# Decoder block on one core: small pads that shift where tiles start within a partition of the on-chip memory

## Chip, cores and metric

The kernel runs on one core of one Trainium2 chip. The time is device microseconds of that core, the median of several executions. The profile is one profiled execution of the same program; its span goes from the first to the last instruction.

## What is computed

A decoder block in float32 over 256 tokens of width 2048: a gated feed-forward layer of width 5632, a token-mixing part (differential attention beside a gated linear recurrence, merged by gates), a second feed-forward layer, and a gated per-layer embedding. Cut to the products that matter for the time:

```python
x = x + 0.5 * swiglu(rmsnorm(x, ffn1_norm), w_gate1, w_up1, w_down1)
h = rmsnorm(x, mix_norm)
dq, dk, dv, hq, hf, hi, hg, gate_a, gate_b = split(h @ w_in)
y_a = diff_attention(dq, dk, dv, ...)
y_b = hgrn2(hq, hf, hi, hg, ...)
merged = sigmoid(gate_a) * (y_a @ w_branch_a) + sigmoid(gate_b) * (y_b @ w_branch_b)
x = x + merged @ w_out
x = x + 0.5 * swiglu(rmsnorm(x, ffn2_norm), w_gate2, w_up2, w_down2)
x = x + sigmoid(rmsnorm(x, ple_gate_norm) @ w_ple_gate) * rmsnorm(p @ w_ple_proj, ple_post_norm)
```

## The kernel before

All weights come once from the main memory, in one stream of 805 groups of two k-tiles (a tile of 128 rows by 512 columns each), in the order of use. `prep` (L101) loads a group into `raw` by a DMA from SP's queue (L112), rounds it on ScalarE into `wh` (L114) and puts the rest, `raw - wh`, into `wl` on VectorE (L115). It runs three groups ahead of the matmuls.

The activations lie transposed, features on partitions, and are split into a rounded and a rest part in the same way: `AH, AL` (16 k-tiles of 256 tokens) after each norm, `hH, hL` for the hidden layer, `yaH, yaL` and `ybH, ybL` for the two branches, `mH, mL` for the merged branch, `pH, pL` for the embedding. `group` (L141) multiplies a group: for each of its two k-tiles and each half of the tokens three matmuls of 128x128 by 128x512. The activation is the **stationary** operand, which a weight load brings into the array, and the weight tile is the **moving** one:

```python
hi, lo = AH[:, kt, tcol(tt)], AL[:, kt, tcol(tt)]
nc.tensor.matmul(dst, hi, wh[:, k2, cols], start=(kt == 0), stop=False)    # L148
nc.tensor.matmul(dst, hi, wl[:, k2, cols], start=False, stop=False)        # L149
nc.tensor.matmul(dst, lo, wh[:, k2, cols], start=False, stop=(kt == last)) # L150
```

So a group is 12 matmuls. In the profile a matmul is listed as out<-moving,stationary: `acc<-wh,AH` is L148 with `AH` stationary. Between two groups of the stream `advance` (L129) issues one piece of every side task: transposes and splits of the hidden layer (L259 to L269), the residual and its transposes (L228), the attention heads, the recurrence (whose small float32 matmuls stand at L589, L616, L629 and L638 to L641).

The order on every engine is that in which the code is written. Tiles are taken from pools; where a tile lies is fixed by the sizes of the tiles allocated before it, each rounded up to 32 bytes, so that the sizes of small tiles decide at what byte the large ones begin. Of the tiles that the three matmuls read, these are the addresses (bytes within a partition, as the built program has them) and what they leave when divided by 128:

| tile | role | address before | mod 128 |
|---|---|---|---|
| `wh` (4 buffers, 4096 bytes apart) | moving | 93248 | 64 |
| `wl` (4 buffers, 4096 bytes apart) | moving | 109632 | 64 |
| `AH`, `AL` | stationary | 34816, 51200 | 0, 0 |
| `hH`, `hL` | stationary | 126016, 171072 | 64, 64 |
| `yaH`, `yaL` | stationary | 150592, 158784 | 64, 64 |
| `ybH`, `ybL` | stationary | 175200, 183392 | 96, 96 |
| `mH`, `mL` | stationary | 191584, 207968 | 96, 96 |
| `pH`, `pL` | stationary | 136256, 138304 | 64, 64 |

The 128 columns of one stationary operand are 512 bytes, and consecutive ones lie 512 bytes apart; a moving operand is 2048 bytes. So each operand has the remainder of its tile.

Of the kernel before, what the change touches and what calls it, by code (L numbers as in the profile page):

```python
# [20 lines left out]
P = 128  # L21
# [27 lines left out]
def block_kernel(ctx: ExitStack, tc: tile.TileContext, a: dict, out: bass.AP):  # L49
# [3 lines left out]
    base = ctx.enter_context(tc.tile_pool(name="base", bufs=1))  # L53
# [8 lines left out]
    def T(pool, shape, tag, dt=F32, **kw):  # L62
        uid[0] += 1
        return pool.tile(shape, dt, tag=tag, name=f"{tag}_{uid[0]}", **kw)
# [4 lines left out]
    def ccol(c):  # L69
        return slice(c * NB, (c + 1) * NB)  # L70

# [1 line left out]
    plan = []  # L73

    def add(w, chunks, groups):
# [39 lines left out]
            nc.vector.tensor_tensor(wl[:, ks, :], raw[:, ks, :], wh[:, ks, :].bitcast(F32), op=ALU.subtract)  # L115
        ready[n] = (wh, wl)

# [1 line left out]
    tasks = []  # L119
    owed = [False]  # L120

# [55 lines left out]
                group(at[0] + i, act, 2 * groups - 1, [d])  # L177
            yield d

# [1 line left out]
    def split(H, L, src, gain=None):  # L181
        if gain is None:
            nc.scalar.copy(H, src)  # L183
            nc.vector.tensor_tensor(L, src, H.bitcast(F32), op=ALU.subtract)  # L184
        else:
            nc.scalar.activation(H, src, AF.Copy, scale=gain)  # L186
            nc.vector.scalar_tensor_tensor(L, src, gain, H.bitcast(F32), op0=ALU.mult, op1=ALU.subtract)
# [34 lines left out]
    def new_act():  # L222
        return T(base, [P, KD, SEQ], "AH", F32R), T(base, [P, KD, SEQ], "AL", F32R)

    def new_ss4():
        return T(base, [P, NT, 4], "ss4", bufs=2)
# [20 lines left out]
    def ffn(gu, down, act, gain_next):  # L247
        with tc.tile_pool(name=gu, bufs=1) as fp:
            hH = T(fp, [P, DFF // P, SEQ], "hH", F32R)
            hL = T(fp, [P, DFF // P, SEQ], "hL", F32R)  # L250

            def hidden(acc, c):
                if c == 0 and rs[0] is None:
                    early = T(fp, [P, NT, NB], "early")
                    for tt in range(NT):
                        nc.scalar.copy(early[:, tt, :], acc[tt])
                    acc = [early[:, tt, :] for tt in range(NT)]
                while rs[0] is None:
                    yield  # L259
                h = []  # L260
                for tt in range(NT):
                    s = T(fp, [P, HALF], "s", bufs=2)
                    nc.scalar.activation(s, acc[tt][:, :HALF], AF.Silu, scale=rs[0][:, tt : tt + 1])  # L263
                    h.append(T(fp, [P, HALF], "h", bufs=4))
                    nc.vector.scalar_tensor_tensor(  # L265
                        h[tt], acc[tt][:, HALF:], rs[0][:, tt : tt + 1], s, op0=ALU.mult, op1=ALU.mult
                    )
                yield
                two_k_tiles(lambda tt, kt: h[tt][:, (kt - 2 * c) * P : (kt - 2 * c + 1) * P], hH, hL, 2 * c)  # L269

            for c in range(DFF // HALF):
                acc = product(gu, c, KG, act)
                spawn(hidden(acc, c))
            nact = new_act()
            ss4 = new_ss4()
            for c in range(D // NB):
                acc = product(down, c, FG, (hH, hL))
                spawn(residual(acc, c, 0.5, ss4, nact, gain_next, set_rs if c == 3 else None))
        return nact

    # ------------------------------------------------------------------ first FFN
    gains = T(base, [P, 4, KD], "gains")
    nc.sync.dma_start(gains, a["gains"])
    neghalf = T(base, [P, 16], "neghalf")
# [7 lines left out]
    small = T(base, [P, 4], "small")  # L292
    ident = T(base, [P, P], "ident")
    x = T(base, [P, NT, D], "x")
    act = new_act()
    ss4 = new_ss4()

    def load_xT(g):
# [26 lines left out]
    spawn(first_sums())  # L325
    act = ffn("gu1", "down1", act, gains[:, G_MIX])

    # ------------------------------------------------------------------ token mixing
    mid = ctx.enter_context(ExitStack())
    mp = mid.enter_context(tc.tile_pool(name="mid", bufs=1))  # L330
    GA = T(mp, [P, NT, D], "GA")
    V = T(mp, [P, NT, NH * VD], "V")
    yaH = T(mp, [P, NH, SEQ], "yaH", F32R)
    yaL = T(mp, [P, NH, SEQ], "yaL", F32R)
    gsub = T(mp, [P, 1], "gsub")
    nc.vector.tensor_scalar(gsub, small[:, S_SUB : S_SUB + 1], 1.0 - LAMBDA_INIT, None, op0=ALU.mult)

    def mix(m):
# [27 lines left out]
    with tc.tile_pool(name="att", bufs=1) as ap:  # L366
        qT = T(ap, [P, NH, SEQ], "qT")
        kT = T(ap, [P, NH, SEQ], "kT")
        dv = T(ap, [P, NT, NH * VD], "dv")
        bias = T(ap, [P, NH, SEQ], "bias")  # L370
# [55 lines left out]
                yield  # L426
            have.add(key)

        # the queries of a tile stand in reversed order from qT to aT, as the rows of the bias do
        PARTS = ((0, slice(0, SEQ), slice(0, SEQ)), (1, slice(SEQ, 3 * P), slice(P, SEQ)))  # L430

        def head(h, ya):
# [304 lines left out]
            spawn(residual(acc, c, 1.0, ss4, act, gains[:, G_FFN2], set_rs if c == 3 else None))  # L737
    mid.close()

    # ------------------------------------------------------------------ second FFN  # L740
    act = ffn("gu2", "down2", act, gains[:, G_PLE])

    # ------------------------------------------------------------------ per-layer embedding
    with tc.tile_pool(name="ple", bufs=1) as pp:
        pT = T(pp, [P, 2, SEQ], "pT")
        nc.gpsimd.dma_start(pT, a["pT"])
# [49 lines left out]
        drain()  # L796


# [1 line left out]
def _blocks(w):  # L800
    k, n = w.shape
    return np.ascontiguousarray(w.reshape(k // (2 * P), 2, P, n // NB, NB).transpose(3, 0, 2, 1, 4))


def _gate_up(gate, up):
    k, n = gate.shape
    both = np.stack([gate.reshape(k, n // HALF, HALF), up.reshape(k, n // HALF, HALF)], axis=2)
    return _blocks(both.reshape(k, 2 * n))


def _feature_major(w):
    n, m = w.shape
    return np.ascontiguousarray(w.reshape(n // P, P, m).transpose(1, 0, 2))
# [12 lines left out]
def _constants():  # L826
    j = np.arange(TOEP)
    dist = SEQ - 1 - j
    hot = np.zeros((BUCKETS + 1, TOEP), np.float32)
    ok = dist >= 0  # L830
    hot[_buckets(dist)[ok], j[ok]] = 1.0
    hot[BUCKETS, ~ok] = NEG
    s = np.arange(P)[:, None]
    t = np.arange(64)[None, :]
    masks = np.stack([(s // (2 * m) == t // m) & (s % (2 * m) < m) for m in LEVELS], axis=1).astype(np.int32)
    return hot, masks


def _layout(v):
    v = {k: np.asarray(w) for k, w in v.items()}  # L840
    hot, masks = _constants()
    f = lambda w: np.ascontiguousarray(w)  # noqa: E731
    x = v["x"][0]
    gains = np.stack([v[n][0].reshape(KD, P).T for n in ("ffn1_norm", "mix_norm", "ffn2_norm", "ple_gate_norm")], axis=1)
    small = np.stack(
        [np.tile(v["q_norm"][0], 2), np.tile(v["k_norm"][0], 2), v["diff_subln"][0], v["hgrn_norm"][0]], axis=1
    )
    return {
        "xT": _feature_major(f(x.T)),
        "x": f(x),  # L850
        "pT": _feature_major(f(v["p"][0, 0].T)),
        "gains": f(gains),
        "small": f(small),
        "ident": np.eye(P, dtype=np.float32),
        "flip": f(np.eye(P, dtype=np.float32)[::-1]),
        "rel_bias": f(v["rel_bias"]),
        "onehot": hot,
        "masks": masks,
        "lambdas": f(np.stack([v[n][0] for n in ("lambda_q1", "lambda_q2", "lambda_k1", "lambda_k2")])),
        "lb": f(v["hgrn_lb_logits"].reshape(2, NH, P).transpose(2, 0, 1)),  # L860
        "ple_post": f(v["ple_post_norm"][0]),
        "gu1": _gate_up(v["ffn1_w_gate"][0], v["ffn1_w_up"][0]),
        "down1": _blocks(v["ffn1_w_down"][0]),
        "w_in": _blocks(v["w_in"][0]),
        "w_a": _blocks(v["w_branch_a"][0]),
        "w_b": _blocks(v["w_branch_b"][0]),
        "w_out": _blocks(v["w_out"][0]),
        "gu2": _gate_up(v["ffn2_w_gate"][0], v["ffn2_w_up"][0]),
        "down2": _blocks(v["ffn2_w_down"][0]),
        "w_pg": _blocks(v["w_ple_gate"][0]),  # L870
        "w_pp": _blocks(v["w_ple_proj"][0]),
    }


def build(arrays):
    import concourse.bacc as bacc

    nc = bacc.Bacc("TRN2", target_bir_lowering=False, num_devices=1)
    aps = {
        n: nc.dram_tensor(f"in_{n}", w.shape, mybir.dt.from_np(w.dtype), kind="ExternalInput").ap()  # L880
        for n, w in arrays.items()
    }
    out = nc.dram_tensor("out_y", (SEQ, D), F32, kind="ExternalOutput").ap()
    with tile.TileContext(nc) as tc:
        block_kernel(tc, aps, out)
    return nc
# [9 lines left out]
```

## Time and profile before

| | before |
|---|---|
| median of 3 executions | 2321.66 us |
| lowest, highest | 2320.70, 2322.68 us |
| profiled execution, first to last instruction | 2320.3 us |
| TensorE (PE) matmul busy | 2312.7 us |
| weight loads (PEld) busy | 1903.2 us |
| VectorE (DVE) busy | 1270.9 us |
| ScalarE (ACT) busy | 1042.7 us |
| GpSimd (POOL) busy | 39.5 us |

For the profiled execution only its span is known; the median of the runs lies 1.4 us above it. The table of stages below comes from the timeline: when the first matmul with each stationary operand of the stream begins.

| first matmul at, us | stationary | product |
|---|---|---|
| 5.51 | AH, AL | first gate and up |
| 502.91 | hH, hL | first down |
| 745.77 | AH, AL | mixing input, with attention and recurrence beside it |
| 1200.30 | yaH, yaL | branch a |
| 1248.84 | AH, AL and ybH, ybL in turn | gate b and branch b, four times |
| 1385.75 | mH, mL | mixing output |
| 1478.82 | AH, AL | second gate and up |
| 1972.69 | hH, hL | second down |
| 2215.52 | AH, AL, twice pH, pL | embedding gate and embedding |

Matmuls are pipelined, and the recorded duration of one runs past the start of the next. The pace is therefore read from the distance between starts, not from the durations.

### The profile page before, as it was taken

The numbers are of one execution on the slowest core, as the hardware profiler recorded it, in microseconds if no ns is written. First come the engines' busy times: TensorE is split into PE (matmuls) and PEld (weight loads), VectorE is DVE, ScalarE is ACT, GpSimd is POOL, SyncE is SP. The second block draws the span as 40 slices with busy tenths as digits, with TensorE's granted clock in tenths as the row PEclk, the third lists the DMA queues.
The fourth block names the chain that finished last, engine by engine and source line by source line (L and its number), as shares of the span: only waits on it lengthen the run. The fifth ranks groups of instructions, "written<-read, shape, count | busy, mean of one in ns | idle before, by whom it ended". The sixth has DMA issues, their size and how long they took to land.

```text
span 2320.3 us, 27206 instructions
## 1 busy us (share of the span) xinstructions
PE 2312.7 (100%) x10564; PEld 1903.2 (82%) x10564; DVE 1270.9 (55%) x1381; ACT 1042.7 (45%) x1270; POOL 39.5 (2%) x38
## 2 busy tenths in 40 slices
PE   9999999999999999999999999999999999999999
PEld 7888888888888888888888888888888888888887
DVE  5554555554444576667765555555555554444456
ACT  6444444444444455543344444544444444444454
POOL 0000000000000100000010000000000000000000
PEclk9999999999999999999999999999999999999999
DMA  8655555566666645554455655565555556666664
GB/s 292 190 182 191 190 188 185 189 189 188 188 188 196 201 161 167 186 173 153 160 156 181 186 186 181 179 193 184 189 190 185 188 188 190 193 188 191 188 213 149
DMA packets 120464, 432.55 MB, mean 186 GB/s; under 512 B 13773, under 2 KB 14181, under 8 KB 120208
## 3 DMA queue, kind: packets, MB, share of 16 engines
q1 hardware_dynamic: 118800, 426.33, 58.3%
q0 software_dynamic: 1248, 4.43, 0.5%
q8 instruction: 82, 1.34, 0.2%
q14 instruction: 46, 0.38, 0.0%
q10 hardware_dynamic: 288, 0.07, 0.0%
HBM read 428.67 MB, written 2.11 MB: 186 GB/s over the span
## 4 chain that ended last, share of the span: by engine, by line
PE 99%; DMA 1%; DVE 0%; ACT 0%; SPq 0%; issue 0%; ACTq 0%; DVEq 0%
PE acc L148 32%; PE acc L150 31%; PE acc L149 31%; PE tp L209 1%; PE ms L616 1%; DMA raw<-in_gu 0%; PE tp L219 0%; PE ms L440 0%; PE ms L150 0%; PE ms L149 0%; PE ms L148 0%; PE ms L589 0%; PE tp L362 0%; DMA junk<-in_xT 0%; PE tp L477 0%; PE ms L641 0%
## 5 line engine op out<-in xcount | busy, mean ns | idle before, releaser
L115 DVE TENSOR_TENSOR wl<-raw,wh 128x1024 fp32r<-128x1024 f32 (+1 forms) x805 | 983.9, 1223 | 888.9 <-ACT wh L114 886.5
L114 ACT CAST wh<-raw 128x1024 fp32r<-128x1024 f32 (+1 forms) x805 | 844.9, 1051 | 941.1 <-PE acc L150 915.6
L148 PE MATMUL acc<-wh,AH 128*128 128x512 f32 x2224 | 885.2, 398 | 0.2 <-ACT wh L114 0.2
L150 PE MATMUL acc<-wh,AL 128*128 128x512 f32 x2224 | 872.3, 392 | 0.0
L149 PE MATMUL acc<-wl,AH 128*128 128x512 f32 x2224 | 866.9, 390 | 1.6 <-DVE wl L115 1.6
L150 PEld LDWEIGHTS acc<-wh,AL 128*128 128x128 f32 x2224 | 417.7, 188 | 95.5
L149 PEld LDWEIGHTS acc<-wl,AH 128*128 128x128 f32 x2224 | 418.1, 188 | 91.5 <-DVE wl L115 3.7
L148 PEld LDWEIGHTS acc<-wh,AH 128*128 128x128 f32 x2224 | 418.4, 188 | 84.7 <-ACT wh L114 1.7
L148 PE MATMUL acc<-wh,hH 128*128 128x512 f32 x704 | 275.3, 391 | 0.0
L150 PE MATMUL acc<-wh,hL 128*128 128x512 f32 x704 | 274.2, 390 | 0.0
L149 PE MATMUL acc<-wl,hH 128*128 128x512 f32 x704 | 273.9, 389 | 0.0
L150 PEld LDWEIGHTS acc<-wh,hL 128*128 128x128 f32 x704 | 132.1, 188 | 27.8
L149 PEld LDWEIGHTS acc<-wl,hH 128*128 128x128 f32 x704 | 132.2, 188 | 27.1
L148 PEld LDWEIGHTS acc<-wh,hH 128*128 128x128 f32 x704 | 132.2, 188 | 27.1
L263 ACT ACTIVATE s<-acc,rowr 128x256 f32<-128x256 f32 x86 | 40.8, 477 | 49.9 <-PE acc L150 49.9
L183 ACT CAST hH<-tp 128x512 fp32r<-128x512 f32 x44 | 25.8, 587 | 74.7 <-PE tp L209 74.7
L184 DVE TENSOR_TENSOR hL<-tp,hH 128x512 fp32r<-128x512 f32 x44 | 30.4, 692 | 46.6 <-ACT hH L183 46.5
L265 DVE SCALAR_TENSOR_TENSOR h<-acc,rowr,s 128x256 f32<-128x256 f32 x86 | 41.4, 483 | 20.6 <-ACT s L263 20.6
L148 PE MATMUL acc<-wh,mH 128*128 128x512 f32 x128 | 51.3, 401 | 0.0
L149 PE MATMUL acc<-wl,mH 128*128 128x512 f32 x128 | 50.6, 395 | 0.0
L150 PE MATMUL acc<-wh,mL 128*128 128x512 f32 x128 | 50.6, 395 | 0.0
L186 ACT ACTIVATE AH<-tp,gains 128x256 fp32r<-128x256 f32 x48 | 22.9, 477 | 31.0 <-PE tp L209 16.9
(191 smaller groups left out, 1019.9 us busy)
## 6 DMA issues: line engine op xcount, KB each, us to landing
raw<-in_gu SPq DMA_DIRECT2D x351, 512.0 KB, 3.5
raw<-in_down SPq DMA_DIRECT2D x176, 512.0 KB, 3.8
raw<-in_w_in SPq DMA_DIRECT2D x176, 512.0 KB, 3.6
raw<-in_w_out SPq DMA_DIRECT2D x32, 512.0 KB, 3.7
raw<-in_w_pg SPq DMA_DIRECT2D x32, 512.0 KB, 4.3
raw<-in_w_a SPq DMA_DIRECT2D x16, 512.0 KB, 3.5
raw<-in_w_b SPq DMA_DIRECT2D x16, 512.0 KB, 3.5
junk<-in_xT SPq DMA_DIRECT2D x8, 256.0 KB, 4.2
```

The lines of the kernel that those rows point to most:

```text
L114: nc.scalar.copy(wh[:, ks, :], raw[:, ks, :])
L115: nc.vector.tensor_tensor(wl[:, ks, :], raw[:, ks, :], wh[:, ks, :].bitcast(F32), op=ALU.subtract)
L148: nc.tensor.matmul(dst, hi, wh[:, k2, cols], start=(kt == 0), stop=False)
L149: nc.tensor.matmul(dst, hi, wl[:, k2, cols], start=False, stop=False)
L150: nc.tensor.matmul(dst, lo, wh[:, k2, cols], start=False, stop=(kt == last))
L183: nc.scalar.copy(H, src)
L184: nc.vector.tensor_tensor(L, src, H.bitcast(F32), op=ALU.subtract)
L186: nc.scalar.activation(H, src, AF.Copy, scale=gain)
L209: nc.tensor.transpose(tp[:, i, tcol(tt)], src_of(tt, kt + i), ident)
L263: nc.scalar.activation(s, acc[tt][:, :HALF], AF.Silu, scale=rs[0][:, tt : tt + 1])
L265: nc.vector.scalar_tensor_tensor(h[tt], acc[tt][:, HALF:], rs[0][:, tt : tt + 1], s, op0=ALU.mult, op1=ALU.mult)
L616: nc.tensor.matmul(lp[:, i, tt, :], km[:, i, tt, :], q4[:, i, tt, :], start=True, stop=True)
```

## The change

A tile of 64 bytes is allocated ahead of `AH, AL` and another one behind them, and nothing reads or writes them. `gsub`, one value per partition, takes a tile of 128 bytes of which one column is used. The other lines of the diff take comments out.

```diff
@@ -292,7 +292,9 @@
     ident = T(base, [P, P], "ident")
     x = T(base, [P, NT, D], "x")
+    T(base, [P, 16], "lead")
     act = new_act()
+    T(base, [P, 16], "trail")
     ss4 = new_ss4()
@@ -325,14 +327,14 @@
     yaL = T(mp, [P, NH, SEQ], "yaL", F32R)
-    gsub = T(mp, [P, 1], "gsub")
+    gsub = T(mp, [P, 32], "gsub")[:, 0:1]
     nc.vector.tensor_scalar(gsub, small[:, S_SUB : S_SUB + 1], 1.0 - LAMBDA_INIT, None, op0=ALU.mult)
```

Names apart, the instructions of every engine and their order stay the same. The addresses become:

| tile | before, mod 128 | after | after, mod 128 | distance to `wh`, mod 512, before | after |
|---|---|---|---|---|---|
| `wh` | 64 | 93376 | 64 | | |
| `wl` | 64 | 109760 | 64 | | |
| `AH`, `AL` | 0 | 34880, 51264 | 64 | 448 | 384 |
| `hH`, `hL` | 64 | 126144, 171200 | 64 | 0 | 0 |
| `yaH`, `yaL` | 64 | 150720, 158912 | 64 | 0 | 0 |
| `ybH`, `ybL` | 96 | 175424, 183616 | 64 | 32 | 128 |
| `mH`, `mL` | 96 | 191808, 208192 | 64 | 32 | 128 |
| `pH`, `pL` | 64 | 136384, 138432 | 64 | 0 | 0 |

The last two columns are the address of the stationary tile less that of `wh`, divided by 512; `wl` lies 16384 bytes behind `wh`, and every step from operand to operand is a multiple of 512, so the remainder is the same for all matmuls of a row.

Of the small float32 matmuls, the recurrence's stationary tiles `k`, `km`, `A` and `off` go from 0 to 96 (and their moving `q`, `qm` from 0 to 96 too, while `V` stays at 64), `qT` and `kT` from 96 to 64, `aT` from 32 to 0 and its moving `dv` from 96 to 64. `x` and `ident`, which the transposes read, stay at 0.

## The prediction

> **What bounds the kernel now.** I read first the page's busy shares, the clock and the chain of work that ended last, to see which engine sets the end.
>
> ```profile
> span 2320.3 us, 27206 instructions
> PE 2312.7 (100%) x10564; PEld 1903.2 (82%) x10564; DVE 1270.9 (55%) x1381; ACT 1042.7 (45%) x1270; POOL 39.5 (2%) x38
> ...
> PEclk9999999999999999999999999999999999999999
> ...
> q1 hardware_dynamic: 118800, 426.33, 58.3%
> ...
> PE 99%; DMA 1%; DVE 0%; ACT 0%; SPq 0%; issue 0%; ACTq 0%; DVEq 0%
> ```
>
> TensorE is busy from end to end at the full granted clock, and 99% of the chain is its own work. VectorE stands at 55%, ScalarE at 45%, the weight queue at 58.3% of the DMA engines. The end moves only if the matmuls follow each other at another pace. Next, the costliest groups, for the kinds of matmul and whether they wait.
>
> ```profile
> L115 DVE TENSOR_TENSOR wl<-raw,wh 128x1024 fp32r<-128x1024 f32 (+1 forms) x805 | 983.9, 1223 | 888.9 <-ACT wh L114 886.5
> L114 ACT CAST wh<-raw 128x1024 fp32r<-128x1024 f32 (+1 forms) x805 | 844.9, 1051 | 941.1 <-PE acc L150 915.6
> L148 PE MATMUL acc<-wh,AH 128*128 128x512 f32 x2224 | 885.2, 398 | 0.2 <-ACT wh L114 0.2
> L150 PE MATMUL acc<-wh,AL 128*128 128x512 f32 x2224 | 872.3, 392 | 0.0
> L149 PE MATMUL acc<-wl,AH 128*128 128x512 f32 x2224 | 866.9, 390 | 1.6 <-DVE wl L115 1.6
> L150 PEld LDWEIGHTS acc<-wh,AL 128*128 128x128 f32 x2224 | 417.7, 188 | 95.5
> ...
> L150 PEld LDWEIGHTS acc<-wh,hL 128*128 128x128 f32 x704 | 132.1, 188 | 27.8
> ...
> L148 PE MATMUL acc<-wh,mH 128*128 128x512 f32 x128 | 51.3, 401 | 0.0
> ```
>
> Three things are to be seen. The matmuls hardly wait for another engine (0.2 and 1.6 us in all). ScalarE's casts wait for TensorE to release `wh` (915.6 us), so the suppliers are ahead. And the recorded 390 to 401 ns of a matmul is no pace, since 6672 of them alone would exceed the span: they overlap. A weight load is recorded with 188 ns whether it reads `AL` (remainder 0) or `hL` (64), so a load's own duration doesn't tell an address apart either.
>
> The pace has to come from starts. The timeline of TensorE gives the starts of single matmuls. I took stretches with nothing but the three lines of the stream, one for each kind of stationary operand, and show the first and last row of each; the remainder of the operand's address is in the tables above.
>
> ```profile
> 259.63 0.40 PE L149 MATMUL acc<-wl,AH 128*128 128x512 f32 x1
> ...
> 281.15 0.39 PE L150 MATMUL acc<-wh,AL 128*128 128x512 f32 x1
> ...
> 509.76 0.39 PE L149 MATMUL acc<-wl,hH 128*128 128x512 f32 x1
> ...
> 547.84 0.39 PE L149 MATMUL acc<-wl,hH 128*128 128x512 f32 x1
> ...
> 1221.48 0.39 PE L149 MATMUL acc<-wl,yaH 128*128 128x512 f32 x1
> ...
> 1248.26 0.39 PE L150 MATMUL acc<-wh,yaL 128*128 128x512 f32 x1
> ...
> 1272.27 0.40 PE L148 MATMUL acc<-wh,ybH 128*128 128x512 f32 x1
> ...
> 1283.24 0.40 PE L150 MATMUL acc<-wh,ybL 128*128 128x512 f32 x1
> ...
> 1415.72 0.40 PE L149 MATMUL acc<-wl,mH 128*128 128x512 f32 x1
> ...
> 1434.86 0.39 PE L150 MATMUL acc<-wh,mL 128*128 128x512 f32 x1
> ...
> 2243.87 0.39 PE L148 MATMUL acc<-wh,AH 128*128 128x512 f32 x1
> ...
> 2265.62 0.39 PE L150 MATMUL acc<-wh,AL 128*128 128x512 f32 x1
> ```
>
> From first to last start, divided by the steps between them:
>
> - `AH` (remainder 0): 95 starts, 21.52 us / 94 = 228.9 ns; in the last stage 96 starts, 21.75 / 95 = 228.9 ns.
> - `hH` (64): 169 starts, 38.08 / 168 = 226.7 ns.
> - `yaH` (64): 119 starts, 26.78 / 118 = 226.9 ns.
> - `ybH` (96): 48 starts, 10.97 / 47 = 233.4 ns.
> - `mH` (96): 83 starts, 19.14 / 82 = 233.4 ns.
>
> ```profile
> 1200.30:1248.80 48.50, 48.50 (x238) 40.86 (x237) 31.07 (x48) 18.93 (x21) 8.21 (x4) 1.00 0.56 173
> 1272.20:1283.40 11.20, 11.20 (x50) 9.02 (x49) 5.12 (x5) 5.06 (x6) 0.00 (x0) 1.00 0.62 185
> ```
>
> These are two windows, of `yaH` and of the first `ybH`: the stretch, its length, the busy time of PE, PEld, DVE, ACT and POOL, the granted clock, the DMA engines' share and GB/s.
>
> So the kernel before already holds an experiment. Shape, types, code lines and moving tiles are the same throughout; the pace falls into three classes, and they go with the remainder: 226.8, 228.95 and 233.4 ns. It isn't the stage: `AH` has one pace beside the hidden layer's work at 260 us and in the quiet stage at 2244 us, while `yaH` and `ybH`, 50 us apart at the same clock, differ by 6.5 ns, and the faster one has the busier neighbour (VectorE 31.07 of 48.5 us against 5.12 of 11.2).
>
> **The change, part by part.** No instruction is added, removed or moved; only starting bytes differ. Each term is a count of matmuls by a difference of pace.
>
> 1. `AH, AL` go from 0 to 64. Three rows of x2224 are 6672 matmuls. If they take the pace of the class at 64, each gains 228.95 − 226.8 = 2.15 ns: **14.3 us**.
>
> ```profile
> L150 PE MATMUL acc<-wh,ybL 128*128 128x512 f32 x64 | 25.3, 396 | 0.0
> ```
>
> 2. `mH, mL` (three lines of x128, 384) and `ybH, ybL` (three of x64, 192) go from 96 to 64: 576 × 6.6 ns = **3.8 us**.
>
> 3. `hH`, `yaH`, `pH` stay at 64, and `wh`, `wl` with them: **nothing**.
>
> 4. The start. In the chain of waits the first groups stand behind their loads:
>
> ```profile
> 5.78 5.35 DMA raw<-in_gu
> ...
> 12.74 5.56 DMA raw<-in_gu
> ```
>
> Up to about 18 us the pace is that of the DMA, and some 60 matmuls gain nothing: 60 × 2.15 ns = **0.1 us** off the sum, 0.2 with the waits just behind.
>
> 5. The small float32 matmuls of recurrence and attention change their remainders, some to 96. The trace of before doesn't show them there.
>
> ```profile
> L616 PE MATMUL ms<-qm,km 128*128 128x64 f32 x192 | 22.7, 271 | 0.0
> ...
> L589 PE MATMUL ms<-q,k 128*128 128x128 f32 x32 | 4.2, 274 | 0.0
> ...
> L477 PE MATMUL tp<-dv,aT 128*128 128x128 f32 x16 | 3.1, 275 | 0.0
> L641 PE MATMUL ms<-V,A 128*128 128x128 f32 x16 | 3.1, 275 | 0.0
> ```
>
> With the other groups of this kind (32 more at L616, 64 at L629 to L641, 16 more with `aT`) they are some 350. If each lost what the worst class of the stream loses against the best, 6.6 ns, that is 2.3 us; if each gained it, −2.3 us. Their recorded durations lie within 271 to 275 ns whether their operands now stand at 0 and 0, at 0 and 64, or at 32 and 96, which is nearest to **no change**: I take 0 and keep both ends.
>
> 6. The 96 narrower matmuls of the last product (L148 to L150 into `ms`, 256 columns) also read `AH, AL`. Bounds are none and the full 2.15 ns, 0.2 us; I take none.
>
> Sum: 14.3 + 3.8 − 0.2 = 17.9 us. The profiled execution would go from 2320.3 to 2302.4 us, and the median, 1.4 us above the span now as then, from 2321.7 to **2303.8 us** (0.8% less).
>
> What is late next? A group takes TensorE 12 × 228.95 = 2.75 us and would take 2.72. The cast takes 1.05 us (L114) and the rest 1.22 (L115) of that, and the queue needs 58.3% of the DMA engines, so the cover stays: nothing that feeds the stream is near its limit. If it were gone, the gain would turn into waits at L148 and L149, which now have 1.8 us.
>
> [...]
>
> **The rivals.**
>
> *The pace follows the distance between stationary and moving operand, with a period longer than 128 bytes* (slower). In the table all operands of the fast class lie at a distance from `wh` that is 0 modulo 512, not only modulo 128. `AH` goes from 448 to 384, `mH` and `ybH` from 32 to 128; none of them reaches 0. With a period of 256 or 512 they may land on a bad distance. The worst pace seen is 233.4 ns; at that, `AH` loses 4.45 ns × 6672 = 29.7 us, and `mH`, `ybH` stay as they are: 2351 us. It is slower as soon as `AH`'s runs lie above 228.95 ns by more than the 0.57 ns that the second term pays for (3.8 us / 6672). For it: the trace has no pair at 128 or 384. Against it: within a class consecutive operands differ by multiples of 512 without a difference in pace, so no longer period than 512 is possible, and the two slow classes differ as much by absolute remainder as by distance; 128 is the shortest period that tells all three apart.
>
> *The same, but neutral for `AH`*: at 384 it keeps 228.95 ns, while `mH` and `ybH` leave the worst place and reach 226.8 to 228.95. The gain is 576 × 4.45 to 6.6 ns = 2.6 to 3.8 us: 2318 to 2319 us, within what can't be told from no change.
>
> *Addresses don't matter; the class is of the product*, by its surrounding work or how its operand was written. Then nothing moves: 2321.7 us. For it: each product has one pace only. Against it: `yaH`, `pH` and `hH` come from three kinds of work and have one pace, `ybH` and `mH` another. [...]
>
> *The second term alone fails, or the first is only halved* (a partial effect at the new distances): 2307 to 2311 us.
>
> **How the numbers follow.** Forecast 0.79, 2303.8 us. Slower by a longer period 0.05; neutral for `AH` 0.08; no effect of addresses 0.04; partial 0.04. Its own bounds: per matmul the classes are known to about 0.1 ns from each side, so the first term is 6672 × 1.95 to 2.25 = 13.0 to 15.0 us and the second 3.7 to 3.9; with the ends of part 5 the gain is 14.2 to 21.4 us. That is 2300.3 to 2307.5 us. To leave out no more than 2 in 10 the range takes the near end of the partial case: 2300 to 2308.5 us. About 0.2% (4.6 us) is what a measurement of this kernel can tell from no change. Faster by more: the forecast and the partial case, 0.83. Within: the neutral case and no effect, 0.12. Slower: 0.05.
>
> **What would show it.** In the changed kernel's timeline, stretches of the stream between two transposes should give 226.6 to 227.0 ns per start for `AH`, `mH` and `ybH` as for `hH`, and `hH` itself should stay. The waits at L148 and L149 should stay near 2 us and the granted clock at full. The slower case shows as `AH` above 229 ns, the neutral one as `AH` at 228.9 with `mH` faster; a pace of 226.8 without a shorter span would mean that the gain turned into a wait. If starts at L589 to L641 stood further apart than before, by 6.6 ns each, part 5 would sit at its upper end.

## Result and profile after

The changed kernel takes 2347.39 us (median of 4 runs, 2345.69 to 2347.81) against 2321.53 us before: a ratio of 1.0108, with a 95% interval of 1.0096 to 1.0120. The forecast was 2303.8 us. It went the other way, and close to the first rival (2351 us). Two of the ten executions of one experiment below, `e4_gsub_only`, took 4715 and 10792 us, its profiled one among them, so that paces aren't read from its trace.

The page of the changed kernel, in the order in which the page of before was read:

```profile
span 2343.6 us, 27206 instructions
PE 2336.3 (100%) x10564; PEld 1905.0 (81%) x10564; DVE 1271.4 (54%) x1381; ACT 1039.7 (44%) x1270; POOL 39.4 (2%) x38
...
PEclk9999999999999999999999999999999999999999
...
L148 PE MATMUL acc<-wh,AH 128*128 128x512 f32 x2224 | 888.5, 400 | 0.6 <-ACT wh L114 0.6
L149 PE MATMUL acc<-wl,AH 128*128 128x512 f32 x2224 | 878.3, 395 | 0.9 <-DVE wl L115 0.9
...
L150 PEld LDWEIGHTS acc<-wh,AL 128*128 128x128 f32 x2224 | 418.4, 188 | 99.3
```

TensorE is busy for 23.6 us more. VectorE and ScalarE are within 3 us of what they were, the waits at L148 and L149 stay small (0.6 and 0.9 us, before 0.2 and 1.6), the clock is full, and a weight load is still recorded with 188 ns. So nothing new is waited for: the matmuls themselves follow each other more slowly. The timeline of TensorE shows which; first and last row of stretches as before.

```profile
262.26 0.39 PE L149 MATMUL acc<-wl,AH 128*128 128x512 f32 x1
...
284.11 0.39 PE L150 MATMUL acc<-wh,AL 128*128 128x512 f32 x1
...
576.02 0.39 PE L149 MATMUL acc<-wl,hH 128*128 128x512 f32 x1
...
632.71 0.39 PE L150 MATMUL acc<-wh,hL 128*128 128x512 f32 x1
...
1284.34 0.40 PE L148 MATMUL acc<-wh,ybH 128*128 128x512 f32 x1
...
1295.31 0.39 PE L150 MATMUL acc<-wh,ybL 128*128 128x512 f32 x1
...
1405.65 0.39 PE L149 MATMUL acc<-wl,mH 128*128 128x512 f32 x1
...
1424.78 0.39 PE L150 MATMUL acc<-wh,mL 128*128 128x512 f32 x1
```

`AH`: 95 starts, 21.85 us / 94 = 232.4 ns (before 228.9). `hH`: 251 starts, 56.69 / 250 = 226.8. `ybH`: 48 starts, 10.97 / 47 = 233.4. `mH`: 83 starts, 19.13 / 82 = 233.3, both as before although their remainder changed from 96 to 64. All of them now start at 64 modulo 128, and still there are a fast and a slow class.

The table sums all steps, worked out from the starts in the two traces. A step goes from the start of one matmul to the start of the next. The first 33 us are left out, and of the stream's own steps those over 255 ns, which hold a stall. The last row has all other matmuls among themselves, transposes and the narrower ones of the last product with them.

| steps with | before | after |
|---|---|---|
| `AH`, `AL` | 6324 steps, 1448.4 us, mean 229.0 ns | 6321 steps, 1471.9 us, mean 232.9 ns |
| `hH`, `hL` | 2084, 473.0, 227.0 | 2084, 472.9, 226.9 |
| `mH`, `mL` | 368, 85.8, 233.3 | 368, 85.8, 233.2 |
| `ybH`, `ybL` | 192, 44.8, 233.4 | 192, 44.8, 233.3 |
| all other matmuls among themselves | 799, 87.4 | 799, 87.4 |

`AH` alone accounts for 23.5 us, and the span grew by 23.3.

### The profile page after: what moved, and what is told of

The parts are those of the page before. It is cut to its first block, busy times and chain, and to the rows that moved or that the text cites. A ratio compares the mean times of both kernels' runs of the same rounds, so it can differ in the third digit from the quotient of the medians.

```text
span 2343.6 us, 27206 instructions
## 1 busy us (share of the span) xinstructions
PE 2336.3 (100%) x10564; PEld 1905.0 (81%) x10564; DVE 1271.4 (54%) x1381; ACT 1039.7 (44%) x1270; POOL 39.4 (2%) x38
## 4 chain that ended last, share of the span: by engine, by line
PE 99%; DMA 1%; DVE 0%; ACT 0%; SPq 0%; issue 0%; ACTq 0%
PE acc L148 31%; PE acc L150 31%; PE acc L149 31%; PE tp L209 1%; PE ms L618 1%; DMA junk<-in_xT 1%; PE tp L219 0%; DMA raw<-in_gu 0%; PE ms L442 0%; PE ms L149 0%; PE ms L150 0%; PE ms L148 0%; PE ms L591 0%; PE tp L364 0%; DVE AL L187 0%; ACT AH L186 0%
## 5 line engine op out<-in xcount | busy, mean ns | idle before, releaser
L148 PE MATMUL acc<-wh,AH 128*128 128x512 f32 x2224 | 888.5, 400 | 0.6 <-ACT wh L114 0.6
L149 PE MATMUL acc<-wl,AH 128*128 128x512 f32 x2224 | 878.3, 395 | 0.9 <-DVE wl L115 0.9
L150 PE MATMUL acc<-wh,AL 128*128 128x512 f32 x2224 | 878.2, 395 | 0.0
L150 PEld LDWEIGHTS acc<-wh,AL 128*128 128x128 f32 x2224 | 418.4, 188 | 99.3
L148 PEld LDWEIGHTS acc<-wh,AH 128*128 128x128 f32 x2224 | 418.7, 188 | 96.6 <-ACT wh L114 1.8
L149 PEld LDWEIGHTS acc<-wl,AH 128*128 128x128 f32 x2224 | 418.8, 188 | 96.3 <-DVE wl L115 2.1
L148 PE MATMUL acc<-wh,hH 128*128 128x512 f32 x704 | 275.3, 391 | 0.0
L150 PE MATMUL acc<-wh,hL 128*128 128x512 f32 x704 | 274.1, 389 | 0.0
L149 PE MATMUL acc<-wl,hH 128*128 128x512 f32 x704 | 273.9, 389 | 0.0
L150 PEld LDWEIGHTS acc<-wh,hL 128*128 128x128 f32 x704 | 132.1, 188 | 27.6
L148 PEld LDWEIGHTS acc<-wh,hH 128*128 128x128 f32 x704 | 132.2, 188 | 27.2
L149 PEld LDWEIGHTS acc<-wl,hH 128*128 128x128 f32 x704 | 132.2, 188 | 27.0
L148 PE MATMUL acc<-wh,mH 128*128 128x512 f32 x128 | 51.2, 400 | 0.0
L150 PE MATMUL acc<-wh,mL 128*128 128x512 f32 x128 | 50.6, 395 | 0.0
L149 PE MATMUL acc<-wl,mH 128*128 128x512 f32 x128 | 50.5, 395 | 0.0
```

## Experiments

Distances below are always the address of a stationary tile less that of `wh`. Every pace is worked out like those above, from the starts of matmuls.

**Everything shifted together, everything at 0, and the change's two halves.** Theory D: the pace hangs on the distance between the stationary and the moving operand.

`e1_shift_all`:
```diff
     x = T(base, [P, NT, D], "x")
+    T(base, [P, 16], "lead")
     act = new_act()
```


> One pad of 64 bytes ahead of AH and nothing else: AH, wh, wl and all that lies behind them move up together by 64 bytes, so every distance between a stationary operand and wh stays as in the kernel before (AH 448, ybH and mH 32, the others 0, modulo 512) while every address changes. Theory D (the pace hangs on the distance between stationary and moving operand, with a period of 256 or 512 bytes): paces stay 229.0 (AH), 226.8 (hH), 233.4 ns (ybH, mH), median 2321.5 us within 2 us. Theory A (the pace hangs on where an operand itself starts): AH now starts at 64 and wh at 0 modulo 128, AH leaves 229.0 ns, and the median moves by 14 us or more one way or the other.

Measured: 2321.71 us, ratio 0.9998 (0.9989 to 1.0007). Its timeline, first and last row of 95 starts with `AH` and of 48 with `ybH`:

```profile
259.10 0.40 PE L149 MATMUL acc<-wl,AH 128*128 128x512 f32 x1
...
280.63 0.39 PE L150 MATMUL acc<-wh,AL 128*128 128x512 f32 x1
...
1271.65 0.40 PE L148 MATMUL acc<-wh,ybH 128*128 128x512 f32 x1
...
1282.62 0.40 PE L150 MATMUL acc<-wh,ybL 128*128 128x512 f32 x1
```

21.53 / 94 = 229.0 ns and 10.97 / 47 = 233.4 ns: every address that the stream reads moved by 64 bytes, `AH` now starts at 64 modulo 128 and `wh` at 0, and no pace moved. It is not where an operand itself starts.

`e2_all_zero`:
```diff
     act = new_act()
+    T(base, [P, 104], "trail")
+    gsub = T(base, [P, 1], "gsub")
     ss4 = new_ss4()
...
-    gsub = T(mp, [P, 1], "gsub")
```


> A pad of 416 bytes behind AL, with gsub (32 bytes) next to it instead of in the mixing pool: every stationary operand of the stream lies at a distance of 0 modulo 512 from wh and wl; all of them start at 0 modulo 128. Theory D: all paces 226.8 ns; AH gains 2.15 ns x 6672, ybH and mH 6.6 ns x 576, together 18 us: median 2303.5 us (2301 to 2306). Theory P (AH, ybH and mH are slower products for a reason of their own, and the shift only made AH worse): AH 229 ns or more, median 2318 us or more.

Measured: 2307.46 us, ratio 0.9936 (0.9922 to 0.9949). First and last row of 95 starts with `AH`, and of 48 with `ybH`:

```profile
257.63 0.40 PE L149 MATMUL acc<-wl,AH 128*128 128x512 f32 x1
...
278.98 0.39 PE L150 MATMUL acc<-wh,AL 128*128 128x512 f32 x1
...
1266.22 0.39 PE L148 MATMUL acc<-wh,ybH 128*128 128x512 f32 x1
...
1276.87 0.39 PE L150 MATMUL acc<-wh,ybL 128*128 128x512 f32 x1
```

21.35 / 94 = 227.1 ns and 10.65 / 47 = 226.6 ns. `AH` and `ybH` reach the fast class, so they were no slower products by nature. The gain, 14.7 us by the medians, is short of the 18 expected; by the sum over steps `ybH` and `mH` gave 3.4 of 3.8 us, `AH` only 10.6 of 14.3. The starts tell why. The mean step with `AH` by its place behind the last break (a step of over 255 ns, or any matmul that isn't of the stream) is, in ns,

```
distance of AH         steps 1-6   7-12   13-18   19-24   61 and later
448 (before)               230.3  228.8   228.9   228.9   228.8
384 (changed kernel)       232.7  232.9   232.9   232.8   232.8
  0 (e2_all_zero)          231.7  228.0   226.7   226.7   226.7
```

At distance 0 a stretch, a run of the stream's matmuls without a break, must first settle: in none of the 96 stretches of more than 20 steps in this run does a step behind the ninth reach 230 ns. The first twelve steps, 1368 of the 6323, take 230.0 ns on average, no less than the 229.6 of the kernel before; at 2.15 ns each they are 2.9 of the 3.7 us that are missing. The break itself isn't needed for it: in the changed kernel `pH` (distance 0) follows `AH` (384) with no other matmul between, and its first nine steps still take 224 to 236 ns before 227 sets in; where `AH` lies at 0 too, `pH` takes 226 or 227 ns from its first step on.

`e3_lead_trail_only` and `e4_gsub_only` are the change's two `T(base, ...)` lines alone and its `gsub` line alone.

> The change without the pad in gsub: AH at distance 384 as in the changed kernel, ybH and mH at 32 as before. Theory D: AH 232.9 ns, the whole loss is here, 3.9 ns x 6672 = 26 us: median 2347.5 us (2345 to 2350). If gsub's part cost anything by itself, the median would be lower than that of the changed kernel by as much.

> The pad in gsub alone: ybH and mH at distance 128 instead of 32 from wh, and the small operands of the recurrence 96 bytes further on; AH and wh as before. Theory D with the paces seen in the changed kernel (233.3 to 233.4 ns at 128, 233.4 at 32): no change, median 2321.5 us within 2 us. By the prediction's second term (remainder 64 modulo 128 is fast) it would be 3.8 us faster.

Measured: 2345.03 us, ratio 1.0099 (1.0085 to 1.0113), and 2321.33 us, ratio 0.9996 (0.9987 to 1.0006). The loss comes with the pads at `AH`, as expected; of the two it is the one behind `AL`, between `AH` and `wh`, since the one ahead of `AH` alone moved nothing (`e1_shift_all`). The first median lies 2.4 us below that of the changed kernel, but the executions overlap (2344.07 to 2346.97 against 2345.69 to 2347.81 us), and the two profiled spans are 2344.1 and 2343.6 us: no cost of `gsub`'s part is shown. Its pad alone moves nothing, and in the changed kernel `ybH` and `mH` only went from one slow distance to another (233.4 ns at 32, 233.3 at 128).

**Which distances are fast.** Pads give each product another distance. The two kernels are the kernel before with these pads, in bytes, ahead of or behind the tiles named:

```diff
     act = new_act()
+    T(base, [P, 48], "trail")           # s2: 120
...
+            if {"gu1": 64, "gu2": 96}[gu]:                              # s2: 288, 320
+                T(fp, [P, {"gu1": 16, "gu2": 24}[gu]], "hpad")          # s2: 72, 80
             hH = T(fp, [P, DFF // P, SEQ], "hH", F32R)
...
+    T(mp, [P, 40], "ypad")              # s2: 88, and gsub [P, 16]
     yaH = T(mp, [P, NH, SEQ], "yaH", F32R)
...
+        T(gp, [P, 8], "mpad")
         mH = T(gp, [P, KD, SEQ], "mH", F32R)
```

> Pads that put each product's stationary operand at another distance from wh, modulo 512: AH 256, hH 64 in the first down product and 96 in the second, yaH 160, ybH 192, mH 224; pH stays at 0. Known so far: 0 gives 226.8 ns, 32 233.4, 128 233.3, 384 232.8, 448 229.0. Theory D with a period of 256: AH at 226.8 ns, ybH (192, the same as 448) at 229.0. Theory D with a period of 512: AH and ybH slow, about 233 ns. Either way hH at 64 and 96 and yaH at 160 about 233 ns. Median with period 256 about 2334 us, with period 512 about 2376 us.

> The same with AH 480, hH 288 and 320, yaH 352, ybH 416, mH 448. Theory D: mH at 448 has AH's 229.0 ns of the kernel before (a theory by which each product has its own curve would leave it elsewhere), AH at 480 lies between 226.8 and 229.0. With a period of 256, 288 and 320 repeat 32 and 64 (233 ns), 352 repeats 96 and 416 repeats 160; with 512 nothing is known of them, about 233.

First and last row of 95 starts with `AH` (256), 251 with `hH` (96), 48 with `ybH` (192) in the first of the two:

```profile
257.72 0.39 PE L149 MATMUL acc<-wl,AH 128*128 128x512 f32 x1
...
279.05 0.39 PE L150 MATMUL acc<-wh,AL 128*128 128x512 f32 x1
...
2037.36 0.39 PE L149 MATMUL acc<-wl,hH 128*128 128x512 f32 x1
...
2095.92 0.40 PE L150 MATMUL acc<-wh,hL 128*128 128x512 f32 x1
...
1273.70 0.39 PE L148 MATMUL acc<-wh,ybH 128*128 128x512 f32 x1
...
1284.46 0.39 PE L150 MATMUL acc<-wh,ybL 128*128 128x512 f32 x1
```

21.33 / 94 = 226.9 ns at 256; 58.56 / 250 = 234.2 at 96; 10.76 / 47 = 228.9 at 192. In the second kernel, 83 starts with `mH` at 448 repeat what `AH` had there:

```profile
1416.22 0.40 PE L149 MATMUL acc<-wl,mH 128*128 128x512 f32 x1
...
1435.00 0.39 PE L150 MATMUL acc<-wh,mL 128*128 128x512 f32 x1
```

18.78 / 82 = 229.0 ns. All distances of the runs so far, mean steps from the thirteenth of each stretch on:

| distance mod 256 | 0 | 32 | 64 | 96 | 128 | 160 | 192 | 224 |
|---|---|---|---|---|---|---|---|---|
| seen at 0 to 255, ns | 226.7 | 233.3 | 233.3 | 234.3 | 233.3 | 233.2 | 228.9 | 233.3 |
| seen at 256 to 511, ns | 226.7 | 233.3 | 233.3 | 234.4 | 232.9 | 233.2 | 228.9 | 233.3 |

The second row repeats the first within 0.4 ns, whichever product was there: the period is 256 bytes. One expectation misses: `AH` at 480 was to lie between 226.8 and 229.0 ns and has 233.3, so the pace doesn't fall off evenly around 0. One execution each took 2326.45 and 2361.48 us, against 2322.24 us of the kernel before; the 2334 us expected of the first counted the 2112 matmuls with `hH` once for each of the two down products, while the two share them.

**Which of the two operands meet.** All at 0, but in the first down product `hL` alone at 128, in the second `hH` alone (pads of 128 ahead of `hL`; of 128 ahead of `hH` and 384 ahead of `hL`).

> All distances 0 as in the run with everything at 0, but in the first down product hL alone is moved to 128, and in the second hH alone. Theory L (the load of the next stationary operand reads beside the stream of the running matmul): in the first down product only the step from L149 to L150 (wl streams while hL loads) rises, by about 6.5 ns or more, and the other two stay at 226.8; in the second the steps from L148 and from L150 rise. Theory O (a matmul's own two operands decide): the risen step is the one that starts at L150 in the first, those at L148 and L149 in the second. Sum over a triple about +6.5 ns in the first and +13 in the second either way.

Mean steps in ns, from the starts, by the line of the matmul that the step starts with (one execution, 2318.45 us):

```
                     from L148   from L149   from L150   of three
hH 0, hL 0               227.2       226.7       226.8      680.7   (e2_all_zero)
hH 0, hL 128             227.1       232.4       234.0      693.5
hH 128, hL 0             232.6       232.8       234.8      700.2
```

Neither theory alone: with `hL` off, both the step in which it loads (L149; in the trace of before, load and L149 both start at 576.04 us) and the step in which it is used (L150) rise; with `hH` off all three do. The sums rise by 12.8 and 19.5 ns where 6.5 and 13 were expected. The clearest step is that from L149 in the second row: its own operands lie at 0, and the load of `hL` beside it takes it from 226.7 to 232.4 ns. In these rows a step is fast only if the operand that loads beside it and its own both lie at 0. That a load itself still meets the stream in the step in which its operand is used, or that one slow step throws the next out of place, can't be told apart by this run.

**Closer to 0.** The pair `hH`, `hL` is one tile, whose use starts some bytes in (`yaH`, `yaL` likewise, 8 bytes in; the rest is as in `e2_all_zero`):

```diff
+            off = {"gu1": 4, "gu2": 1}[gu]   # values of 4 bytes
+            both = T(fp, [P, 2 * DFF // P * SEQ + 8], "h2", F32R)
+            both = both[:, off : off + 2 * DFF // P * SEQ].rearrange("p (j k s) -> p j k s", j=2, s=SEQ)
+            hH, hL = both[:, 0], both[:, 1]
```


> All distances 0 but for a start moved inside a larger tile: hH and hL at 16 bytes in the first down product, at 4 bytes in the second, yaH and yaL at 8 (ybH and mH come to lie at 32). If the pace falls off step by step from 0, 4 and 8 bytes stay below 229 ns and 16 lies between 226.8 and 233.4; if a line of 32 or 64 bytes is what counts, all three stay at 226.8; if only an exact match is fast, all are at 233.

First and last row of 263 starts in the first chunk (512 output columns) of the first down product (16 bytes), of 251 in its second chunk, and of 251 in the second product (4 bytes):

```profile
501.19 0.39 PE L149 MATMUL acc<-wl,h 128*128 128x512 f32 x1
...
560.58 0.39 PE L150 MATMUL acc<-wh,h 128*128 128x512 f32 x1
...
564.72 0.40 PE L149 MATMUL acc<-wl,h 128*128 128x512 f32 x1
...
623.05 0.40 PE L150 MATMUL acc<-wh,h 128*128 128x512 f32 x1
...
2032.81 0.39 PE L149 MATMUL acc<-wl,h 128*128 128x512 f32 x1
...
2090.89 0.40 PE L150 MATMUL acc<-wh,h 128*128 128x512 f32 x1
```

59.39 / 262 = 226.7 ns and 58.33 / 250 = 233.3 ns at the same 16 bytes; 58.08 / 250 = 232.3 ns at 4 bytes; `yaH` at 8 bytes has 230.7 ns. The three expectations all miss: there is no slope and no line, 4 bytes cost most of the full price, and at 16 bytes a whole chunk of the product settles in one of two paces (the third chunk has 233.3 ns, the fourth 226.7). The one execution took 2319.28 us.

**Matmuls alone.** Only resident operands, no casts, no transfers:

```python
for i in range(64):
    j = i % 2 * (512 // size)
    nc.tensor.matmul(acc[i % 2], s[:, e + j : e + j + P], m[:, i // 2 % 2, :], start=True, stop=True)
nc.tensor.matmul(brk[:, :64], x[:, 0, 0:P], x[:, 1, 0:64], start=True, stop=True)
```


> Matmuls alone: nothing of the block is computed; two moving operands and one stationary tile are loaded once, then stretches of 64 matmuls of 128x128 by 128x512 follow, each with its stationary operands at another distance from the moving ones (27 distances from 0 to 512 bytes for the rounded float32 type, 9 for bfloat16), a small float32 matmul between stretches, the whole list twice. No cast, no subtraction, no DMA runs beside them. Theory D alone (the load's reads and the stream's reads of TensorE meet): the paces of the block return, 226.8 ns at 0, 256 and 512, 229.0 at 192 and 448, about 233.3 at the others. Theory N (it takes the writes of ScalarE, VectorE or the DMAs into the same memory): all distances have one pace. For bfloat16, whose load reads half the bytes, theory D says only that any difference is smaller.

The program took 1090.68 us, one execution. In its timeline a stretch of 64 is one row: first start, time to the last one's end. The second round, at the distances 0, 4, 8, 128, 192 and 256, then two of bfloat16 (0 and 128):

```profile
544.71 14.80 PE L48 MATMUL acc<-M,S 128*128 128x512 f32 x64
559.49 15.13 PE L48 MATMUL acc<-M,S 128*128 128x512 f32 x64
574.59 15.01 PE L48 MATMUL acc<-M,S 128*128 128x512 f32 x64
...
665.40 15.17 PE L48 MATMUL acc<-M,S 128*128 128x512 f32 x64
...
756.02 14.91 PE L48 MATMUL acc<-M,S 128*128 128x512 f32 x64
...
876.43 14.79 PE L48 MATMUL acc<-M,S 128*128 128x512 f32 x64
...
951.14 13.98 PE L48 MATMUL acc<-MB,SB 128*128 128x512 bf16 x64
...
1007.06 13.98 PE L48 MATMUL acc<-MB,SB 128*128 128x512 bf16 x64
```

Between 0 and 128 lie 15.17 − 14.80 = 0.37 us for 63 steps, 5.9 ns a step, the settling at the start included; over the second half of each stretch the paces are 226.7, 232.4, 230.6, 233.5, 228.8 and 226.7 ns, those of the block. Over this second round the window shows PE and PEld busy, and nothing of VectorE, ScalarE and GpSimd, with the DMA engines' share at 0.00 (the columns as in the windows above):

```profile
544.70:1070.00 525.30, 525.30 (x2346) 386.06 (x2345) 0.00 (x0) 0.00 (x0) 0.00 (x0) 1.00 0.00 1
```

So the effect needs none of these: with them idle the paces are 226.7 ns at 0 and 233.5 at 128, beside them in the block 226.7 and 233.3. With bfloat16 all nine distances take 13.98 us. The expectation "about 233.3 at the others" misses for 4 and 8 bytes, as in the block, and for some of the distances tried only here: 240 has 228.3 ns, 176 230.0, 200 230.7, 208 231.8 and 184 232.0, while 188, 196, 248 and 252 beside them have 233.3. At 16 both rounds have 233.3 ns; the second pace of the block didn't appear.

**The change with a period of 256.**

`e5_pads_256`:
```diff
+    T(base, [P, 16], "lead")
     act = new_act()
+    T(base, [P, 48], "trail")
...
-    gsub = T(mp, [P, 1], "gsub")
+    gsub = T(mp, [P, 64], "gsub")[:, 0:1]
```


> The change with other sizes at its own places: 64 bytes ahead of AH, 192 instead of 64 behind AL, gsub 256 instead of 128. AH, ybH and mH then lie 256 bytes, modulo 512, from wh; the others at 0. With a period of 256: AH about 227.2 to 227.4 ns as in the run with everything at 0, ybH and mH 226.7 to 227.4, median 2307.5 us (2306 to 2309). With a period of 512 it would stay at or above the kernel before, 2321 us or more.

Measured: 2307.42 us, ratio 0.9938 (0.9925 to 0.9952). With other sizes at the same three places the change is faster than the kernel before by 0.6%, and than the changed one by 40 us.

## Why the prediction was wrong

- **What bounds the kernel**: right. TensorE's pace set the end: it is busy for 100% of the span before and after, and in `e2_all_zero`, `e3_lead_trail_only` and `e5_pads_256`, and its work is 99% of the chain that ended last in each. Loss and gain of pace came through to the span: 23.5 us more in the steps of the changed kernel are 23.3 us of span, 14.0 us less in those of `e2_all_zero` are 14.6.
- **The step that failed** is the reading of the classes: "the pace falls into three classes, and they go with the remainder: 226.8, 228.95 and 233.4 ns". The rows were right, but the fast class had two things in common, the remainder 64 modulo 128 and a distance of 0 modulo 512 to `wh`. The remainder was taken as the rule. `e1_shift_all` separates them: it gives `AH` the remainder 64, and `AH` keeps its 229.0 ns.
- **The period of 128 failed with it.** To go by distance would not have been enough: modulo 128 the new distances 384 and 128 are 0 as well, and the forecast would have been the same. The prediction held 128 for good because it "is the shortest period that tells all three apart", which no row demanded. `s1_distances` and `s2_distances` show a period of 256: 384 is slow like 128 (232.9 and 233.3 ns), 256 is fast like 0 (226.7).
- **Part 1** then had the wrong sign: `AH` went from 448 to 384, by the period of 256 from 192 (229.0 ns) to 128 (232.9 ns), and lost 23.5 us in place of a gain of 14.3.
- **Part 2** came to 0 in place of 3.8 us: 32 and 128 cost the same.
- **Parts 3, 5 and 6**: right as far as measured. `hH` and `yaH` kept their pace (226.7 and 226.9 ns before, 226.8 and 226.7 after); the 48 steps with `pH` went from 226.9 to 228.5 ns, the settling behind a slower `AH`, less than 0.1 us. The other matmuls took 87.4 us before and after, and the narrow ones of the last product had 117.8 and 118.2 ns a step, 118.9 with everything at 0.
- **The rivals**: the first named the mechanism, the distance with a longer period than 128, and priced it at 2351 us by the worst pace seen, 233.4 ns; measured were 2347.4 us and 232.9 ns. That the price came so close is partly luck: nothing in the trace of before said that 384 would be near the worst. Its chance of 0.05 was too low. The argument held against it, that the slow classes differ as much by remainder as by distance, spoke for neither. The table of the change said that 128 and 384 were where the operands would go, and the trace of before had no pace for either: the forecast rested on two distances that nobody had seen.
- **The size of the gain**, where it does come (`e2_all_zero`): 14.7 us, not 18. The 226.8 ns were read from long stretches, and the first steps behind each break, which have yet to settle, gain nothing.

Open is how the distance acts: no run shows what in the hardware sets the pace, why 192 (228.9 ns) costs a third of the others (233.3), why 240 and 176 (228.3 and 230.0 ns) are faster than their neighbours (233.3 at 248, 232.0 at 184), and why at 16 bytes a chunk may settle at either pace (226.7 or 233.3 ns).

## What to carry to other kernels

Where matmuls of the rounded float32 type (fp32r in the profile) and of this shape set the end, place the stationary tile and the moving tile at the same address modulo 256 bytes: settled steps took 226.7 ns there, 228.9 to 234.4 at the other multiples of 32 bytes. The distance counts, not the alignment of either: a pad between the two can undo it (32 bytes cost 6.6 ns a step here), a pad ahead of both can't (`e1_shift_all` kept 229.0 and 233.4 ns). When classes in a trace suggest a rule, list every quantity that goes with the classes, and check that the change keeps all of them, not only the one named; where the change leads to a value that the trace doesn't have, the classes say nothing of it. A shift of everything together is a cheap test of absolute against relative.

## What the hardware showed beyond that

- For this type and shape a settled step takes 226.7 ns on average at the best distance and 234.4 ns at the worst (352 bytes); bfloat16 takes 215.8 ns between starts at all nine distances tried.
- The recorded duration of a weight load (188 ns before and after) and the waits at L148 and L149 (0.2 and 1.6 us before, 0.6 and 0.9 after) showed nothing of it, and those of the matmuls little (`wl,AH` 390 ns before, 395 after); the distance between starts showed it.
- At distance 0 the fast pace has to settle: behind a break, or behind a product at another distance, up to nine steps of 224 to 236 ns pass first.
